# A compression MLP inside an attention layer with its matmul operands exchanged: the weights stand still, the windows stream

## The chip, the core and the metric

The kernel runs on one core of a Trainium2 chip. The metric is the device time of one execution in microseconds; lower is better. Five engines matter here: PE (TensorE), DVE (VectorE), ACT (ScalarE), POOL (GpSimd), and SP, which only issues transfers: all of this kernel's loads, stores and moves between tiles stand in SP's one queue, in the order in which the program issues them.

## What is computed

One forward pass in f32 over 512 tokens of width 1024: an even mixer, an MLP, an odd mixer, an MLP, then a hybrid mixer and a gated MLP. The hybrid mixer's second branch attends, per head, to selected keys, to a window of keys, and to keys and values that were compressed from 32 tokens into one. The change touches only the making of these:

```python
def compress(x, pe, w1, w2):
    B, S, G, dh = x.shape
    nc = (S - CMP_LEN) // CMP_STRIDE + 1
    idx = np.arange(nc)[:, None] * CMP_STRIDE + np.arange(CMP_LEN)[None, :]
    blk = x[:, idx] + pe[None, None, :, None, :]
    blk = blk.transpose(0, 1, 3, 2, 4).reshape(B, nc, G, CMP_LEN * dh)
    return jax.nn.silu(blk @ w1) @ w2
...
    k_cmp = compress(apply_rope(kv(kc_), c3, s3), cmp_pe_k, cmp_k_w1, cmp_k_w2)
    v_cmp = compress(kv(vc_), cmp_pe_v, cmp_v_w1, cmp_v_w2)
```

Here S = 512, G = 2 groups, dh = 64, CMP_LEN = 32, CMP_STRIDE = 16. So there are 31 windows for each of 2 groups, 62 in all; w1 is 2048 x 256 and w2 is 256 x 64. The product with w1 is 62 x 2048 x 256, once for k and once for v.

## The kernel before

The program first records its operations without issuing them (class with `own`, `later`, `schedule`, `issue`), then `schedule()` (L391) simulates the engines with costs of its own and writes out one order per engine; then every operation is issued from one line, L372. So every row of the trace has L372, and tiles are told apart by name. Names with several buffers share a pool (`BUFS`, L544): three of P, G and L, two of strip, wr, wh, wl, one of acc and rbcq; in PSUM three of psg (the pool "g", for projections), two each of pss and psp, one of pso. A tile gets a buffer when the last user of an older one is done. Work recorded under `rec.later(LATER)` is filler: it is recorded ahead, with a lower priority than the attention heads whose waits it is to fill.

A projection ("gemm") works in pieces: a weight piece of 512 KB is loaded to wr; ACT copies it to wh in a narrower float format, DVE writes the rest to wl, and each 128 x 512 result in psg takes 24 matmuls, with wh, wh and wl.

The hybrid mixer (L1211) makes, as filler under the first differential attention heads (L1317 to L1349): the projections vc and kcs (what is to be compressed), kw, then `compress("v")` (L1338), the projection nsa_v (L1340: values of both other branches, in four token tiles), `compress("k")` (L1342), and the first query projection nq0 (L1344). After the next heads come nq1 (L1399), the rest of k's compression (`next(hk)`, L1400), and the gate projection mg0, whose first piece is followed by `cmp_tiles` (L1406), which multiplies the compressed hidden states by w2.

`compress` (L1518) is a generator in two halves. The first writes the windows (two strip tiles of 128 x 496: partition = half of a window's 32 positions x 64 features, columns = 8 positions x 62 windows), loads w1 in eight pieces of 256 KB, alternately to rbcq and acc, and multiplies: 16 steps, each with 62 window columns as the stationary operand and 256 columns of weights moving, into psg[62, 256]. The second half computes y * 1/(1+exp(-y)) on 62 partitions x 256, turns it with two PE transposes into 128 x 62 halves, and copies these into `hid` (a P tile). One f32 matmul appears in the trace as two records of PE, each with its own weight load.

The planner's price for an f32 matmul is `max(4n/2.4, 428)` ns, with n the moving columns (L322 and following).

Of the kernel before, what the change touches and what calls it, by code (L numbers as in the profile page):

```python
# [102 lines left out]
def pack_weights(i):  # L103
    pk = Packer()
    r = np.arange
    w = i["w_in_ab"][0]
    o_q, o_k, o_v, o_f, o_qb, o_kb, o_vb = 0, 512, 1024, 1536, 1544, 2056, 2568
    pk.moving("fox_v0", w, np.concatenate([r(o_v, o_v + 256), r(o_f, o_f + 8)]))
    pk.moving("fox_v1", w, r(o_v + 256, o_v + 512))
    for t in range(4):  # L110
        pk.stationary(f"fox_qk{t}", w, np.concatenate([r(o_q + 128 * t, o_q + 128 * t + 128), r(o_k + 128 * t, o_k + 128 * t + 128)]))
        pk.stationary(f"chk_qk{t}", w, np.concatenate([r(o_qb + 128 * t, o_qb + 128 * t + 128), r(o_kb + 128 * t, o_kb + 128 * t + 128)]))
    pk.moving("chk_v0", w, r(o_vb, o_vb + 256))
    pk.moving("chk_v1", w, r(o_vb + 256, o_vb + 512))
    for h in range(2):
        pk.stationary(f"out_ab{h}", i["w_out_ab"][0][512 * h:512 * h + 512])
        pk.stationary(f"out_cd{h}", i["w_out_cd"][0][512 * h:512 * h + 512])
    for l in range(2):
        for s in range(4):
            pk.stationary(f"up{l}_{s}", i["w_up"][l][:, 1024 * s:1024 * s + 1024])  # L120
            pk.stationary(f"down{l}_{s}", i["w_down"][l][1024 * s:1024 * s + 1024])

    w = i["w_in_cd"][0]
    for t in range(4):
        pk.stationary(f"sb_qk{t}", w, np.concatenate([r(128 * t, 128 * t + 128), r(512 + 128 * t, 640 + 128 * t)]))
    pk.moving("sb_v0", w, r(1024, 1280))
    pk.moving("sb_v1", w, r(1280, 1536))
    pk.stationary("cq", w, r(1536, 1920))
    pk.stationary("ckv", w, r(1920, 2176))
    kr = r(2176, 2208)  # L130
    krs = np.concatenate([kr[16:], kr[:16]])
    pk.stationary("kr", w, np.concatenate([kr, krs, kr, krs]))
    w = i["w_uq"][0]
    hd = r(8)[:, None] * 96
    pk.stationary("uq_rope", w, np.concatenate([(hd + 64 + r(16)[None]).reshape(-1), (hd + 80 + r(16)[None]).reshape(-1)]))
    nope = (hd + r(64)[None]).reshape(-1)
    for t in range(4):
        pk.stationary(f"uq_nope{t}", w, nope[128 * t:128 * t + 128])
    w = i["w_ukv"][0]
    hd = r(8)[:, None] * 128  # L140
    kn = (hd + r(64)[None]).reshape(-1)
    vv = (hd + 64 + r(64)[None]).reshape(-1)
    for t in range(4):
        pk.stationary(f"ukv_k{t}", w, kn[128 * t:128 * t + 128])
    for g in range(2):
        pk.moving(f"ukv_v{g}", w, vv[256 * g:256 * g + 256])

    w = i["w_in_2"][0]
    dq, dk, dv, nq, kc, vc, ks, vs, kw, vw, ng, mg = 0, 512, 1024, 1536, 2048, 2176, 2304, 2432, 2560, 2688, 2816, 2840
    pk.stationary("vc", w, r(vc, vc + 128))  # L150
    halves = lambda o, n, b: (o + r(n)[:, None] * 64 + 32 * b + r(32)[None]).reshape(-1)
    for b in range(2):
        pk.stationary(f"kcs{b}", w, np.concatenate([halves(kc, 2, b), halves(ks, 2, b)]))
    pk.stationary("kw", w, np.concatenate([halves(kw, 2, 0), halves(kw, 2, 1)]))
    pk.moving("nsa_v", w, np.concatenate([r(vs, vs + 128), r(vw, vw + 128), r(ng, ng + 24)]))
    for g in range(2):
        for b in range(2):
            pk.stationary(f"nq{g}{b}", w, halves(nq + 256 * g, 4, b))
            pk.stationary(f"dq{g}{b}", w, halves(dq + 256 * g, 4, b))
            pk.stationary(f"dk{g}{b}", w, halves(dk + 256 * g, 4, b))  # L160
        pk.moving(f"dv{g}", w, r(dv + 256 * g, dv + 256 * g + 256))
    for b in range(2):
        pk.stationary(f"mg{b}", w, r(mg + 1024 * b, mg + 1024 * b + 1024))
    pk.stationary("ya", i["w_branch_a_2"][0])
    pk.stationary("yb", i["w_branch_b_2"][0])
    pk.stationary("out2", i["w_out_2"][0])
    for s, f0 in enumerate(range(0, FF2, 1024)):
        f1 = min(f0 + 1024, FF2)
        pk.stationary(f"gate_{s}", i["w_gate_2"][0][:, f0:f1])
        pk.stationary(f"up2_{s}", i["w_up_2"][0][:, f0:f1])  # L170
        pk.stationary(f"down2_{s}", i["w_down_2"][0][f0:f1])
    for n in "kv":
        w1 = i[f"cmp_{n}_w1_2"][0].reshape(2, 16, 64, 256)
        w1 = np.concatenate([w1[0], w1[1]], axis=1)
        pk.plain(f"cmp1{n}", [w1[l:l + 2].transpose(1, 0, 2).reshape(128, 512) for l in range(0, 16, 2)])
    return pk


# [324 lines left out]
class Net:  # L503
# [709 lines left out]
    def hybrid_mixer(self):  # L1213
# [100 lines left out]
            nc.vector.tensor_scalar(z[:, i], ps[:, 256:280], self.rcol[:, i:i + 1], None, ALU.mult)  # L1314

        with self.rec.later(LATER):
            self.gemm("vc", h, evac_vc)  # L1317
            self.gemm("kcs0", h, evac_kcs)
            self.gemm("kcs1", h, evac_kcs)
            a, b = self.rope(hold[0], hold[1], ck[:, 0], ck[:, 1], None)  # L1320
            raw["k"] = self.rows_of(self.tl("QS", [128, 2, 512]))
            for g in range(2):
                r = slice(32 * g, 32 * g + 32)
                for o, src in ((0, a), (32, b)):
                    nc.sync.dma_start(raw["k"][g][o:o + 32], src[r])
                    nc.sync.dma_start(raw["k"][g][64 + o:96 + o, 0:496], src[r, 16:512])
            sa, sb_ = self.pair("AB"), self.pair("AB")
            self.split(sa[64:128], a[64:128])
            self.split(sb_[64:128], b[64:128])
            for g in range(2):  # L1330
                k = self.pair("KK")
                r = slice(64 + 32 * g, 96 + 32 * g)
                for d in (0, 64):
                    self.move(k[d:d + 32], sa[r])
                    self.move(k[d + 32:d + 64], sb_[r])
                ksel.append(k)
            self.gemm("kw", h, evac_kw)
            hv = self.compress("v", raw["v"])  # L1338
            next(hv)
            vt = self.v_tiles("nsa_v", h, rcol, gates)  # L1340
            hv = next(hv)
            hk = self.compress("k", raw["k"])  # L1342
            next(hk)
            qs0 = self.roped_stacks("nq0", h, cq, "QS")  # L1344
            nc.scalar.activation(z, z, AF.Exp, scale=-1.0)
            nc.vector.tensor_scalar(z, z, 1.0, None, ALU.add)
            nc.vector.reciprocal(gt, z)
            late = self.tl("P", [128, 256])
            nc.sync.dma_start(late, self.ins["late"][:, 256:512])  # L1349
            self.cmask = self.c2("cmask", self.tl("cmask", [128, 128]))  # L1350
# [164 lines left out]
        self.gemm_tok(key, stat, evac)  # L1515
        return res

    def compress(self, n, src):  # L1518

        nc = self.nc  # L1520
        win = []
        for l0 in (0, 8):
            t = self.tl("strip", [128, 8, 2, 31])
            pe = self.v(f"pe{n}")[:, l0:l0 + 8].unsqueeze(2).to_broadcast([128, 8, 31])
            for g in range(2):
                view = src[g][:, 0:496].rearrange("p (c l) -> p l c", l=16)
                nc.vector.tensor_tensor(t[:, :, g], view[:, l0:l0 + 8], pe, ALU.add)
            win.append(t)
        ps = self.psum("g")
        for l in range(16):  # L1530
            if l % 2 == 0:
                off, w = self.pk.index[f"cmp1{n}"][0][l // 2]
                wt = self.tl("acc" if l % 4 else "rbcq", [128, 512])
                nc.sync.dma_start(wt, self.ins["w"][off:off + 128 * w].rearrange("(p c) -> p c", p=128))
            nc.tensor.matmul(ps[0:62, 0:256], win[l // 8][:, l % 8].rearrange("p g c -> p (g c)"),
                             wt[:, 256 * (l % 2):256 * (l % 2) + 256], start=(l == 0), stop=(l == 15))
        yield
        act = self.tl("P", [128, 512])
        e, y = act[0:62, 0:256], act[0:62, 256:512]
        nc.scalar.activation(e, ps[0:62, 0:256], AF.Exp, scale=-1.0)  # L1540
        nc.scalar.activation(y, ps[0:62, 0:256], AF.Copy)
        nc.vector.tensor_scalar(e, e, 1.0, None, ALU.add)
        nc.vector.reciprocal(e, e)
        nc.vector.tensor_tensor(y, y, e, ALU.mult)
        ps = self.psum("g")
        for m in range(2):
            nc.tensor.transpose(ps[:, 64 * m:64 * m + 62], y[:, 128 * m:128 * m + 128], self.c("ident")[0:62, 0:62])
        hid = self.tl("P", [128, 2, 2, 32])
        nc.vector.memset(hid, 0.0)
        for m in range(2):  # L1550
            nc.vector.tensor_copy(hid[:, m, :, 0:31], ps[:, 64 * m:64 * m + 62].rearrange("p (g c) -> p g c", g=2))
        yield hid

    def cmp_tiles(self, hk, hv, late):
# [236 lines left out]
```

## Time and profile before

| | |
|---|---|
| runs of the kernel before | 2073.0, 2075.69, 2075.41 us, median 2075.41 |
| the profiled execution | 2075.91 us; span of the trace 2074.2 us |
| mean granted TensorE clock | 0.991 of full speed |
| busy: PE, its weight loads, DVE, ACT, POOL | 97%, 81%, 55%, 43%, 19% of the span |

How to read it: durations are those of the profiled execution. PE's row counts matmul time, PEld's its weight loads, which overlap with matmuls. A timeline row is a run of equal instructions; in brackets stands how long its engine had been idle before it, and what released it. In an operand list `psg<-rbcq,strip` the tile written comes first, then the moving one, then the stationary one. A tile's two numbers, as in 128*62, are the rows and the columns of the stationary operand. The share of PE leaves 58 us of the span in which it is idle.

### The profile page before, as it was taken

The page shows a single profiled execution, that of the slowest core. Times are in us where ns is not written, and L with a number is a line of the kernel's source. Part 1 is how long each engine was busy: PE and PEld are TensorE (multiplying, and loading weights), DVE is VectorE, ACT ScalarE, POOL GpSimd, SP SyncE. Part 2 cuts the span into 40 slices and gives each one's busy share as a digit, 9 for nine tenths or more (in the row PEclk, how much of TensorE's full clock was granted, in tenths as well). Part 3 has the DMA queues.
Part 4 walks back from the last instruction along what each step waited for, and adds up shares of the span by engine and source line. Part 5 has one row for each costly group of instructions (what it writes and reads, how often), then busy time and mean ns, then how long its engine had stood idle before and what let it go on. Part 6 is the DMA issues. An engine that isn't in the chain of part 4 may idle for free. (4 is left out here: it accounts for less than half of the span.)

```text
span 2074.2 us, 27227 instructions
## 1 busy us (share of the span) xinstructions
PE 2016.1 (97%) x9958; PEld 1684.7 (81%) x9958; DVE 1134.4 (55%) x2033; ACT 895.1 (43%) x1621; POOL 394.3 (19%) x524
## 2 busy tenths in 40 slices
PE   8999999999999998999999999989999999999998
PEld 7887778888888887878888888867788888888887
DVE  6657763434444677874434354766786644333334
ACT  5556542323344565652323253534685543222224
POOL 2343210000022453220000014212240221011013
PEclk9999999999999999999999999999999999999999
DMA  6545623233344325633333334464113222323232
GB/s 199 135 128 152 195 83 102 92 102 92 101 134 132 102 62 130 194 101 96 97 100 94 102 120 141 119 174 126 60 42 112 92 101 92 102 92 102 91 102 82
DMA packets 80677, 231.98 MB, mean 112 GB/s; under 512 B 11552, under 2 KB 15520, under 8 KB 80544
## 3 DMA queue, kind: packets, MB, share of 16 engines
q1 hardware_dynamic: 80544, 230.25, 36.8%
q8 instruction: 78, 1.28, 0.3%
q14 instruction: 55, 0.45, 0.1%
HBM read 183.04 MB, written 10.49 MB: 93 GB/s over the span
## 5 line engine op out<-in xcount | busy, mean ns | idle before, releaser
L372 PE MATMUL psg<-h,wh 128*128 128x512 f32 x2688 | 847.3, 393 | 1.0 <-ACT h L372 0.6
L372 ACT ACTIVATE wh<-wr 128x1024 fp32r<-128x1024 f32 (+3 forms) x313 | 326.2, 1042 | 847.8 <-PE psg L372 679.1
L372 PEld LDWEIGHTS psg<-h,wh 128*128 128x128 f32 x2688 | 503.4, 189 | 101.4 <-ACT h L372 1.1
L372 PE MATMUL psg<-h,wl 128*128 128x512 f32 x1344 | 528.6, 393 | 0.9 <-DVE wl L372 0.7
L372 DVE TENSOR_TENSOR wl<-wr,wh 128x1024 fp32r<-128x1024 f32 (+3 forms) x313 | 385.7, 1233 | 60.7 <-ACT wh L372 59.6
L372 PEld LDWEIGHTS psg<-h,wl 128*128 128x128 f32 x1344 | 253.7, 189 | 53.1 <-DVE wl L372 2.4
L372 DVE TENSOR_TENSOR x<-psg,x 128x512 f32<-128x512 f32 (+1 forms) x120 | 78.1, 654 | 281.9 <-PE psg L372 281.9
L372 PE MATMUL psg<-KK,wh 128*128 128x512 f32 (+1 forms) x752 | 226.3, 382 | 0.0
L372 POOL TENSOR_TENSOR acc<-acc,T 128x512 f32<-128x512 f32 (+1 forms) x50 | 73.5, 1470 | 776.6 <-issue 629.1
L372 PE MATMUL psg<-V,wh 128*128 128x512 f32 (+1 forms) x656 | 200.4, 386 | 0.0
L372 PEld LDWEIGHTS psg<-KK,wh 128*128 128x128 f32 x752 | 140.0, 188 | 27.5
L372 PE MATMUL psg<-KK,wl 128*128 128x512 f32 (+1 forms) x376 | 143.8, 382 | 0.0
L372 PEld LDWEIGHTS psg<-V,wh 128*128 128x128 f32 x656 | 122.8, 188 | 25.0
L372 DVE SCALAR_TENSOR_TENSOR T<-psg,rbc 128x512 f32<-128x512 f32 x64 | 44.3, 692 | 167.8 <-PE psg L372 167.2
L372 PE MATMUL psg<-o,wh 128*128 128x512 f32 x400 | 131.8, 399 | 3.4 <-DVE AB L372 1.5
L372 ACT ACTIVATE x<-x,sm 128x128 f32<-128x128 f32 (+1 forms) x192 | 106.5, 558 | 55.9 <-DVE sm L372 55.5
L372 PE MATMUL psg<-V,wl 128*128 128x512 f32 (+1 forms) x328 | 126.7, 386 | 0.0
L372 PE MATMUL psg<-wh,h 128*128 128x256 f32 (+2 forms) x560 | 113.8, 290 | 6.9 <-ACT wh L372 6.8
L372 PE MATMUL pso<-pt,V 128*128 128x128 f32 (+3 forms) x432 | 108.1, 337 | 2.7 <-ACT pt L372 1.3
L372 POOL TENSOR_SCALAR x<-x,sm 128x128 f32<-128x128 f32 (+1 forms) x112 | 65.4, 589 | 178.5 <-DVE sm L372 100.2
L372 PEld LDWEIGHTS psg<-wh,h 128*128 128x128 f32 x560 | 91.6, 193 | 8.8 <-ACT wh L372 6.8
L372 POOL TENSOR_TENSOR T<-T,rbc 128x512 f32<-128x512 f32 x22 | 39.2, 1781 | 280.5 <-ACT T L372 280.5
(267 smaller groups left out, 2701.4 us busy)
## 6 DMA issues: line engine op xcount, KB each, us to landing
wr<-in_w_dram SPq DMA_DIRECT2D x302, 512.0 KB, 3.5
KK<-AB SPq DMA_DIRECT2D x48, 256.0 KB, 5.6
QS<-AB SPq DMA_DIRECT2D x48, 128.0 KB, 3.8
x<-xs SPq DMA_DIRECT2D x24, 256.0 KB, 3.3
xs<-P SPq DMA_DIRECT2D x16, 256.0 KB, 3.5
xs<-x SPq DMA_DIRECT2D x16, 256.0 KB, 2.0
h<-AB SPq DMA_DIRECT2D x16, 256.0 KB, 3.8
KK<-AB SPq DMA_DIRECT2D x32, 128.0 KB, 2.3
```

The source lines that it names most:

```text
L372: op.inst = getattr(getattr(nc, op.eng), op.name)(*op.args, **op.kw)
```

## The change

w1 is packed anew, as four blocks of 128 x 1024 (512 KB) instead of eight of 128 x 512; each block holds 8 positions for one half (128) of the 256 hidden columns. The blocks go to the three 4 KB buffers of L, which so far only the odd mixer uses. The loads are recorded by a new function, `cmp_weight`: three of v's ahead of the projections, two of k's ahead of nsa_v, the others where their matmuls come. The windows go to the single buffers rbcq and acc, which the weights had. The matmuls exchange their operands: 128 x 128 of weights stand, 62 columns of windows move; there are 32 for each of k and v instead of 16. Their result is 128 x 62, hidden columns on the partitions, so that the two transposes and the two copies go. The activations work on 128 partitions: four of 128 x 62 instead of two of 62 x 256, a reciprocal of 128 x 128 instead of 62 x 256, and two products written straight into `hid`. `hid` is now taken before `act`, both from P, and `act` is cleared too.

```diff
-        pk.plain(f"cmp1{n}", [w1[l:l + 2].transpose(1, 0, 2).reshape(128, 512) for l in range(0, 16, 2)])
+        pk.plain(f"cmp1{n}", [w1[l:l + 8, :, m:m + 128].transpose(1, 0, 2).reshape(128, 1024) for m in (0, 128) for l in (0, 8)])
...
         with self.rec.later(LATER):
+            wv = [self.cmp_weight("v", b) for b in range(3)]
             self.gemm("vc", h, evac_vc)
...
-            hv = self.compress("v", raw["v"])
+            hv = self.compress("v", raw["v"], wv)
             next(hv)
+            wk = [self.cmp_weight("k", b) for b in range(2)]
             vt = self.v_tiles("nsa_v", h, rcol, gates)
             hv = next(hv)
-            hk = self.compress("k", raw["k"])
+            hk = self.compress("k", raw["k"], wk)
...
+    def cmp_weight(self, n, b):
+        off, w = self.pk.index[f"cmp1{n}"][0][b]
+        t = self.tl("L", [128, 1024])
+        self.nc.sync.dma_start(t, self.ins["w"][off:off + 128 * w].rearrange("(p c) -> p c", p=128))
+        return t
...
-            t = self.tl("strip", [128, 8, 2, 31])
+            t = self.tl("acc" if l0 else "rbcq", [128, 512])[:, 0:496].rearrange("p (l g c) -> p l g c", l=8, g=2)
...
-        for l in range(16):
-            if l % 2 == 0:
-                off, w = self.pk.index[f"cmp1{n}"][0][l // 2]
-                wt = self.tl("acc" if l % 4 else "rbcq", [128, 512])
-                nc.sync.dma_start(wt, self.ins["w"][off:off + 128 * w].rearrange("(p c) -> p c", p=128))
-            nc.tensor.matmul(ps[0:62, 0:256], win[l // 8][:, l % 8].rearrange("p g c -> p (g c)"),
-                             wt[:, 256 * (l % 2):256 * (l % 2) + 256], start=(l == 0), stop=(l == 15))
+        for m in range(2):
+            for l in range(16):
+                b = 2 * m + l // 8
+                if b == len(ws):
+                    ws.append(self.cmp_weight(n, b))
+                c = 128 * (l % 8)
+                nc.tensor.matmul(ps[:, 64 * m:64 * m + 62], ws[b][:, c:c + 128],
+                                 win[l // 8][:, l % 8].rearrange("p g c -> p (g c)"), start=(l == 0), stop=(l == 15))
         yield
-        act = self.tl("P", [128, 512])
-        e, y = act[0:62, 0:256], act[0:62, 256:512]
-        nc.scalar.activation(e, ps[0:62, 0:256], AF.Exp, scale=-1.0)
-        nc.scalar.activation(y, ps[0:62, 0:256], AF.Copy)
+        act = self.tl("P", [128, 2, 128])
+        e, y = act[:, 0], act[:, 1]
+        hid = self.tl("P", [128, 2, 2, 32])
+        nc.vector.memset(hid, 0.0)
+        nc.vector.memset(act, 0.0)
+        for m in range(2):
+            c = slice(64 * m, 64 * m + 62)
+            nc.scalar.activation(e[:, c], ps[:, c], AF.Exp, scale=-1.0)
+            nc.scalar.activation(y[:, c], ps[:, c], AF.Copy)
         nc.vector.tensor_scalar(e, e, 1.0, None, ALU.add)
         nc.vector.reciprocal(e, e)
-        nc.vector.tensor_tensor(y, y, e, ALU.mult)
-        ps = self.psum("g")
         for m in range(2):
-            nc.tensor.transpose(ps[:, 64 * m:64 * m + 62], y[:, 128 * m:128 * m + 128], self.c("ident")[0:62, 0:62])
-        hid = self.tl("P", [128, 2, 2, 32])
-        nc.vector.memset(hid, 0.0)
-        for m in range(2):
-            nc.vector.tensor_copy(hid[:, m, :, 0:31], ps[:, 64 * m:64 * m + 62].rearrange("p (g c) -> p g c", g=2))
+            c = slice(64 * m, 64 * m + 62)
+            nc.vector.tensor_tensor(hid[:, m, :, 0:31], y[:, c].rearrange("p (g c) -> p g c", g=2),
+                                    e[:, c].rearrange("p (g c) -> p g c", g=2), ALU.mult)
         yield hid
```

Because the order is planned from costs and buffers, rows move that the diff does not name. In the rows of the planned order a tile has a number, x8 means eight instructions in a row, and the listing's shapes are those of the tile written.

**SP's queue from v's compression to k's.** Before, from the load of v's third piece on (KK and wr belong to the key copies and the next projections):

```order
L372 DMA rbcq_2470<-in_w_dram 128x512
L372 DMA acc_2471<-in_w_dram 128x512
L372 DMA wr_2505<-in_w_dram 128x1024
L372 DMA wr_2509<-in_w_dram 128x1024
L372 DMA KK_2463<-AB_2462 32x1024 x4
L372 DMA KK_2464<-AB_2462 32x1024 x4
L372 DMA rbcq_2472<-in_w_dram 128x512
L372 DMA acc_2473<-in_w_dram 128x512
```

Changed, from the load of v's fourth block (L_2471) to k's last (L_2494); v's first three stand much earlier, in the odd mixer:

```order
L373 DMA L_2471<-in_w_dram 128x1024
L373 DMA wr_2496<-in_w_dram 128x1024
L373 DMA wr_2500<-in_w_dram 128x1024
L373 DMA L_2472<-in_w_dram 128x1024
L373 DMA KK_2466<-AB_2465 32x1024 x4
L373 DMA KK_2467<-AB_2465 32x1024 x4
L373 DMA L_2473<-in_w_dram 128x1024
L373 DMA L_2493<-in_w_dram 128x1024
L373 DMA wr_2604<-in_w_dram 128x1024
L373 DMA wr_2608<-in_w_dram 128x1024
L373 DMA L_2494<-in_w_dram 128x1024
```

v's pieces that stood behind the eight KK moves are gone from there. k's last block stands behind the two wr pieces of nq1 (wr_2604 and wr_2608).

**PE from k's compression to nq0.** Before, the last six k groups and nq0's first result, psg_2504, alternate; k's result is psg_2495:

```order
L372 MATMUL psg_2495<-acc_2501,strip_2494 62x256 x2
L372 MATMUL psg_2504<-h_2203,wl_2507 128x512
L372 MATMUL psg_2504<-h_2210,wh_2506 128x512 x2
L372 MATMUL psg_2504<-h_2210,wl_2507 128x512
L372 MATMUL psg_2504<-h_2217,wh_2506 128x512 x2
L372 MATMUL psg_2504<-h_2217,wl_2507 128x512
L372 MATMUL psg_2504<-h_2224,wh_2506 128x512 x2
L372 MATMUL psg_2504<-h_2224,wl_2507 128x512
L372 MATMUL psg_2495<-rbcq_2502,strip_2494 62x256 x2
L372 MATMUL psg_2495<-acc_2503,strip_2494 62x256 x2
L372 MATMUL psg_2508<-h_2177,wh_2510 128x512 x2
```

Changed (psg_2486 is the last tile of nsa_v, psg_2492 k's result, psg_2495 now nq0's first):

```order
L373 MATMUL psg_2486<-wh_2478,h_2224 128x280
L373 MATMUL psg_2486<-wl_2479,h_2224 128x280
L373 MATMUL psg_2486<-wh_2478,h_2224 128x280
L373 MATMUL psg_2492<-rbcq_2490,L_2472 128x62 x8
L373 MATMUL psg_2492<-acc_2491,L_2473 128x62 x8
L373 MATMUL psg_2492<-rbcq_2490,L_2493 128x62 x8
L373 MATMUL psg_2492<-acc_2491,L_2494 128x62 x8
L373 MATMUL psg_2495<-h_2177,wh_2497 128x512 x2
```

All 32 matmuls of k's compression stand between nsa_v and nq0. k's result is read by ACT only at the place that follows, so that its psg buffer stays taken until then; nq1's first result, psg_2603, follows psg_2495 and psg_2499 with a wait for DVE, which it had not before.

**PE and DVE at `cmp_tiles`.** Before (psg_2638 and psg_2641: v's tiles for the two groups, from strip and w2 in P_2520; pso and psp belong to an attention head):

```order
L372 MATMUL psg_2632<-h_2224,wl_2635 128x512
L372 MATMUL psg_2638<-P_2520,strip_2637 128x64 x2
L372 MATMUL pso_2707<-pt_2669_2741,V_2483 128x512 [waits Activation_49]
L372 MATMUL psp_2744<-cst,x_2735 128x128 [waits DVE_49,PE_49]
L372 MATMUL psp_2744<-cst,x_2738 128x128
L372 MATMUL pso_2707<-pt_2669_2741,V_2483 128x512
L372 MATMUL pso_2707<-pt_2671_2743,V_2485 128x384 [waits Activation_49]
L372 MATMUL psp_2746<-cst,x_2738 128x128 [waits DVE_49,PE_49]
L372 MATMUL pso_2707<-pt_2671_2743,V_2485 128x384
L372 MATMUL pso_2707<-pt_2673_2745,V_2487 128x256 [waits Activation_49]
L372 MATMUL pso_2707<-pt_2673_2745,V_2487 128x256 [waits DVE_49]
```

Changed, PE (psg_2628 and psg_2631 are v's tiles, psg_2633 k's, P_2620 k's `hid`):

```order
L373 MATMUL psg_2622<-h_2224,wl_2625 128x512
L373 MATMUL psg_2628<-P_2511,strip_2627 128x64 x2
L373 MATMUL psg_2631<-P_2511,strip_2630 128x64 [waits DVE_49]
L373 MATMUL psg_2631<-P_2511,strip_2630 128x64
L373 MATMUL psg_2633<-P_2620,P_2511 64x64 [waits DVE_49] x2
L373 MATMUL psg_2636<-o_2385,wh_2638 128x512 [waits Activation_49]
L373 MATMUL psg_2636<-o_2385,wh_2638 128x512
```

Changed, DVE at the same place (P_2489 is v's `hid`, P_2619 k's `act`):

```order
L373 COPY strip_2630<-P_2489 128x2x32 [waits PE_49]
L373 TENSOR_TENSOR wl_2644<-wr_2642,wh_2643 128x1024 [waits DMAHW2_49,Activation_49]
L373 TENSOR_TENSOR vcmp_2557_2629<-psg_2628,vcmp_2557_2629 128x64 [waits Activation_49]
L373 COPY strip_2630<-P_2489 128x2x32 x3
L373 SCALAR_TENSOR_TENSOR V_2621<-V_2621,G_2626 128x512 [waits DVE_49,Activation_49]
L373 MEMSET P_2619 128x256 [waits DVE_49]
L373 TENSOR_SCALAR P_2619<-P_2619 128x128 [waits DVE_49,Activation_49]
L373 TENSOR_TENSOR vcmp_2560_2632<-psg_2631,vcmp_2560_2632 128x64 [waits Activation_49]
L373 RECIPROCAL P_2619<-P_2619 128x128 [waits DVE_49]
L373 TENSOR_TENSOR P_2620<-P_2619 128x2x31 [waits DVE_49]
L373 TENSOR_TENSOR P_2620<-P_2619 128x2x31
```

The attention matmuls that stood between v's two tiles stand earlier now. k's sigmoid, which ran during nq0 and nq1 before, stands between v's second tile and k's product with w2: P_2619 takes the buffer of P_2489, which the copies to strip_2630 read last.

## Rows read from the trace of the kernel before

**Rows 1.** The page, part 1: busy time, share of the span, instructions of TensorE and its weight loads.
```profile
PE 2016.1 (97%) x9958; PEld 1684.7 (81%) x9958; DVE 1134.4 (55%) x2033; ACT 895.1 (43%) x1621; POOL 394.3 (19%) x524
```

**Rows 2.** Stretches of 20 us: busy us of each engine (x instructions), granted clock, DMA share, GB/s.
```profile
1380.00:1400.00 20.00, 13.97 (x85) 11.04 (x83) 10.28 (x37) 7.13 (x19) 2.45 (x4) 0.92 0.61 166
...
1460.00:1480.00 20.00, 19.02 (x86) 15.41 (x84) 11.23 (x39) 7.32 (x23) 1.67 (x3) 0.83 0.19 63
```

**Rows 3.** Timeline of PE, 1372 to 1401: start, duration, group, [idle before <-releaser].
```profile
1372.58 1.08 PE L372 MATMUL psg<-rbcq,strip 128*62 128x256 f32 x4 [1.33 <-DVE strip L372]
...
1374.44 0.40 PE L372 MATMUL psg<-wh,h 128*128 128x280 f32 x1
...
1383.67 1.07 PE L372 MATMUL psg<-rbcq,strip 128*62 128x256 f32 x4 [0.61 <-DMA rbcq<-in_w_dram]
...
1391.32 0.29 PE L372 MATMUL psg<-wh,h 128*128 128x280 f32 x1
1396.93 1.96 PE L372 MATMUL psg<-rbcq,strip 128*62 128x256 f32 x4 [5.32 <-DMA rbcq<-in_w_dram]
...
1400.33 0.74 PE L372 MATMUL pss<-o,X 128*128 128x512 f32 x2
```

**Rows 4.** Timeline of SP's DMA queue, 1381 to 1395: start, time in the queue, transfers.
```profile
1383.63 10.24 SPq L372 DMA_DIRECT2D KK<-AB  x8
1393.96 0.53 SPq L372 DMA_DIRECT2D rbcq<-in_w_dram  x1
```

**Rows 5.** Timeline of PE: small moving tiles, each with the next matmul behind it.
```profile
1416.49 0.94 PE L372 MATMUL pss<-cst,T 128*128 128x1 f32 x8
1417.30 0.48 PE L372 MATMUL psg<-h,wl 128*128 128x512 f32 x1
...
1457.78 0.55 PE L372 MATMUL psg<-P,strip 128*128 128x64 f32 x4
...
1458.31 0.49 PE L372 MATMUL pso<-pt,V 128*128 128x512 f32 x1
```

**Rows 6.** Groups by form, 1365 to 1470, PE: busy us, mean ns | idle before, releaser.
```profile
L372 PE MATMUL psg<-cst,P 62*128 62x62 f32 x4 | 0.9, 258 | 0.0
```

**Rows 7.** The page, part 6: issues, KB each, median us to landing.
```profile
wr<-in_w_dram SPq DMA_DIRECT2D x302, 512.0 KB, 3.5
```

**Rows 8.** Timelines of DVE, ACT and SP around one split of a weight tile.
```profile
1410.61 1.05 ACT L372 ACTIVATE wh<-wr 128x1024 fp32r<-128x1024 f32 x1
...
1411.63 1.21 DVE L372 TENSOR_TENSOR wl<-wr,wh 128x1024 fp32r<-128x1024 f32 x1
...
1412.90 0.33 SPq L372 DMA_DIRECT2D wr<-in_w_dram  x1
...
1426.48 0.69 DVE L372 TENSOR_TENSOR G<-psg,X 128x512 f32<-128x512 f32 x1 [3.39 <-PE psg L372]
```

**Rows 9.** Timeline of all engines, 1459 to 1465, in which k's and v's compressed tiles are made.
```profile
1459.41 0.41 PE L372 MATMUL psp<-cst,x 128*128 128x128 f32 x2 [0.61 <-DVE pt L372]
...
1459.88 1.22 DVE L372 TENSOR_TENSOR wl<-wr,wh 128x1024 fp32r<-128x1024 f32 x1
...
1461.49 0.90 PE L372 MATMUL pso<-pt,V 128*128 128x256 f32 x3 [0.78 <-DVE pt L372]
...
1461.55 0.68 DVE L372 SCALAR_TENSOR_TENSOR V<-V,G 128x512 f32<-128x512 f32 x1
...
1462.59 1.12 PE L372 MATMUL psg<-P,strip 128*128 128x64 f32 x4 [0.20 <-DVE strip L372]
...
1463.64 0.69 PE L372 MATMUL psg<-P,P 128*64 128x64 f32 x4
...
1463.75 0.22 ACT L372 ACTIVATE vcmp<-psg 128x64 fp32r<-128x64 f32 x1 [0.86 <-PE psg L372]
```

**Rows 10.** Groups by form, 1365 to 1470, DVE: busy us, mean ns | idle before, releaser.
```profile
L372 DVE RECIPROCAL P<-P 62x256 f32<-62x256 f32 x2 | 3.4, 1713 | 0.0
```

**Rows 11.** Timeline of PE in the odd mixer, where its three L tiles come free.
```profile
849.09 0.93 PE L372 MATMUL pss<-h,h 96*128 96x128 f32 x6 [2.18 <-DMA h<-AB]
```

More of the change, by code (lines that the diff above doesn't have):

```diff
@@ L1516, in wide_v, with compress @@
         return res
-    def compress(self, n, src):
+    def cmp_weight(self, n, b):
[3 more added lines that the diff above has]
+        return t
+    def compress(self, n, src, ws):
         nc = self.nc
```

## The prediction

> **What bounds the kernel now.** The page's first part says that PE is busy for 97% of the span [rows 1]. So time is won only where PE does less or stands idle, and lost only where PE is made to wait. A difference under about 0.2% (4 us) can't be told from no change here.
>
> The windows over 1380 to 1480 show where PE idles near the change: 6.03 of the 20 us from 1380, and 0.98 from 1460, where the clock is granted at 0.83 [rows 2]. The timeline says why [rows 3]. At 1391.32 PE runs out of work and sits 5.32 us until a rbcq piece of v's weights lands; 0.61 us at 1383.67 have the same releaser. SP's queue shows that this piece was not slow but late: its turn came at 1393.96, behind eight KK moves that held the queue for 10.24 us [rows 4]. The idle stretch costs twice: after it the eight f32 records take 1400.33 - 1396.93 = 3.40 us, where eight took 1374.44 - 1372.58 = 1.86 at the start of v; the clock behind the wait is at half (1.2 GHz), 1.54 us lost. So 5.32 + 0.61 + 1.54 = 7.5 us hang on late weights.
>
> **The matmuls.** Before: 64 records at 1.86 / 8 = 0.2325 us, 14.9 in all at full clock. After: 128 records, each with a load of 128 weight columns and 62 moving columns. The nearest rows: 128 x 128 f32 with one moving column, eight from 1416.49 to 1417.30, 0.101 each; with 64 columns, four from 1457.78 to 1458.31, at most 0.133 each [rows 5]. One column costs three quarters of what 64 do, so the weight load sets the pace. 128 x 0.101 = 12.9 and 128 x 0.133 = 17.0; I take 0.11, nearer to the longer run of eight: 14.1. **Term: -0.8 us, from -2.0 to +2.1.** Double the instructions, a quarter of the columns, the same time.
>
> The four transpose records go: 258 ns each, overlapping [rows 6]; at the pace of the one-column rows 0.1 each. **Term: -0.4.** The four activations more are short (one of 128 x 64 took 0.22 [rows 9]) and ACT is at 43% [rows 1]: nothing by themselves. The reciprocal falls from 1.71 us [rows 10] to about half (128 of 256 columns, 0.86): DVE is at 55%, nothing where it runs under nq0, but it counts below.
>
> **v and nsa_v.** The three blocks of v loaded in the odd mixer are there long before, and the fourth stands before the eight KK moves: the 7.5 us go. Given back: v's matmuls alternated with nsa_v, and both covered the first head's chain of softmax, transposes and products. Now v's matmuls come first and are its only cover. From 1374.44 to 1391.32 stand 54 records of nsa_v [rows 3], 6.9 us at some 0.13 a record (280 columns at 2.4 GHz are 0.12); with 16 of v's records, 3.7 us, that is 10.6 us of cover. After, it is v's 7.05, so 3.5 less. If PE only queued behind filler, nothing is lost (0); if the chain keeps the pace it had, 3.5, and up to 1 more because PE's order is fixed and a wait holds what stands behind it. I take 3: nearly each chain row of PE waits for DVE or ACT in the planned order. **Term: -7.5 + 3.0 = -4.5, from -7.5 to -3.0.**
>
> **k.** k's 32 matmuls stand in one piece after nsa_v. The last block, L_2494, stands in SP's queue behind wr_2608, and this waits for a wr buffer, which is free when wl of nq0's second piece is written, and that needs a wl buffer of nsa_v. From nsa_v's end: evacuation 0.69 (like that of G), wh 1.05, wl 1.21, two issues of 0.33 [rows 8], landing 3.5 [rows 7]: 7.1 us. In the rows the wr issue follows wl's end by 0.06. Three groups of k cover 48 x 0.11 = 5.3. **Term: +1.8, from 0 (if the split starts in nsa_v's last tile) to +3.**
>
> **The psg buffer.** k's result keeps one of three buffers until after nq1, so nq1's first result waits for the two readings of psg_2499 by DVE, 0.69 each [rows 8], and a margin for the hand-over, which no row isolates: **+1.6, from 0 (covered) to +3.3** (if it gets psg_2495's buffer, whose second reader stands behind these, a wl of 1.21 and takes 0.69 itself).
>
> **cmp_tiles.** Before, 4.3 us went from v's first tile to its second (1458.31 to 1462.59), with attention between them, and k's product followed at 1463.64: 5.3 us [rows 5, 9]. After, nothing stands between, and k's sigmoid hangs on the release of v's `hid`. DVE from the first tile on: wl 1.22, two copies and v's difference 0.6, one product 0.68 [rows 9], the memset 0.2, four activations of 0.22 on ACT, an addition 0.3, the reciprocal 0.86, two products 0.35: 5.1, and with hand-overs between PE, DVE, ACT, DVE and PE, which I put at 0.35 each, some 6.5 us. PE's own two tiles cover 1.5 of it, so it idles 5.0. Before, it idled 0.61 + 0.78 + 0.20 = 1.6 here [rows 9]. That is 3.4 more; the attention work moved forward fills some wait of its old neighbours, so I take **+3.0, from +2.0 to +4.5.** In the window with these waits the clock was granted at 0.83 already [rows 2]; a longer stop may keep it at half longer, by what the wait at 1391 cost: **+0.7, from 0 to 1.5.**
>
> **Odd mixer.** Three loads of 512 KB enter SP's queue where the L tiles come free, where PE already waits 2.18 us for a move of h [rows 11]. An issue of a load stayed 0.33 us in the queue [rows 8]; three before such a move are 1 us, none 0, and the transfers share the memory. **+0.5, from -1 (another order, by chance better) to +2.**
>
> **Sum:** -0.8 - 0.4 - 4.5 + 1.8 + 1.6 + 3.7 + 0.5 = **+1.9 us** on the profiled execution's 2075.9. That execution stands 0.5 above the median of the three runs, 2075.4, so I forecast 2077.3: no change that can be measured, with a lean to slower.
>
> **A rule to weigh.** By the one-column rows a record with 128 weight columns takes 0.101 us, however few columns move [rows 5]. The Trainium skill ("TensorE: Matmul & The Clock Gate", section "Back-to-back issue gap") gives an isolated gap of about 60 cycles for 1 to 64 moving columns; by 25 ns a record the 128 would be 3.2 us, and by that the sum would be -9.0, 2066.4. The one-column row contradicts this for f32 with a new weight tile each time, so it is a rival of small chance, below.
>
> **Rivals.**
>
> *A, slower: k's sigmoid on the critical path.* k's hidden state has no slack left; its memset waits for DVE's copies, and PE has nothing else in its order. For it: the planned rows at `cmp_tiles`, and the psg buffer. Against it: attention work moved forward may cover elsewhere. It decides once what it adds, with the buffer and L_2494, passes the 5.7 us won at matmuls, transposes and v by over 4. With cmp_tiles at +4.5 and 1.5 of clock, the buffer at 3.3, the wait for L_2494 at 3 and v at -3.0: -1.2 - 3.0 + 3 + 3.3 + 6 + 0.5 = +8.6, about 2084.0.
>
> *B, faster: late weights were the whole matter.* The 7.5 us come through, because the chain kept its pace only by queueing behind filler, and the waits behind are short: -0.8 - 0.4 - 7.5 + 0.5 + 0.5 + 2 = -5.7, about 2069.7. For it: the 5.32 us are one clean wait [rows 3, 4], and three blocks now land 500 us early. Against it: each of the new waits would have to come in at its low end.
>
> *C, faster: moving columns set the time.* 62 of 256 columns of 0.2325 us are 0.056 a record, 7.2 us in all instead of 14.1: the sum falls to -5.0, about 2070.4. The one-column row speaks against it. This is the case that the rule above is nearest to.
>
> *D, the change does not do what it says.* The planner prices an f32 matmul at no less than 428 ns, so 64 of them count 27 us for it where the rows say 14; it may have placed all else for a PE that is later than it is, and the wait for DMA only moves, from v's rbcq to k's L_2494, at 5 us and half clock after it: -1.2 - 4.5 + 5 + 1.5 + 1.6 + 3.7 + 0.5 = +6.6, 2082.0.
>
> **How the numbers follow.** My forecast (within 0.2%) 0.42; A 0.20 and D 0.13, both slower, 0.33 together; B 0.20 and C 0.05, both faster, 0.25. The range goes from below B to above A, since these hold more than half of the chance and neither end can be left out: 2067.5 to 2085.5. The likeliest case alone would be 2071.3 to 2079.5.
>
> **What would show it.** Right: PE's records of psg<-rbcq,L and psg<-acc,L start 0.10 to 0.13 us apart; no PE wait for a weight DMA in v, a short one before k's last group; a wait for DVE before psg of nq1; idle of some 5 us before psg<-P,P, released by DVE P. Wrong: records under 0.08 or over 0.15 us apart; gaps in v over 5 us; psg<-P,P starting without a wait; or a difference of over 3 us that lies before 1365 or after 1480.

## The result and the profile after

| | before | changed |
|---|---|---|
| median of 17 runs, us | 2073.0 (2066.5 to 2077.4) | 2084.2 (2080.2 to 2096.3) |
| ratio, 95% interval | | 1.0064, 1.0050 to 1.0079 |
| profiled execution: span, mean granted clock | 2074.2, 0.991 | 2094.4, 0.983 |

The change makes the kernel slower by 0.64%, some 13 us. The forecast was no measurable change. The page of the changed kernel, part 1, answers to [rows 1]:

```profile
PE 2028.8 (97%) x10018; PEld 1706.6 (81%) x10018; DVE 1134.1 (54%) x2033; ACT 895.1 (43%) x1625; POOL 394.4 (19%) x524
```

PE is busier by 12.7 us, although it has less to stream: the first sign that its time at half clock grew, and not its work.

The profiled execution of the change was the slowest of its 17, and 3.5 us of its distance lie before 846 us, where both kernels issue the same orders; 7.9 in all have come together by the end of kw. The prediction named a difference of over 3 us ahead of 1365 as a sign of being wrong. It isn't shown to come from the change: some 0.7 of it arises where the three early loads stand (840 to 856), and with the same loads v starts 1.4 and 4.4 us earlier than before in the profiles of e2 and e8 (below). From the end of kw the distance grows to 20.1 us at 1490, and stays there to the end. So the change is worth about +12.2 us in the stretch of compression, which agrees with the ratio. Over the 17 runs of the change the time follows the mean granted clock: 0.981 to 0.985 in the six slowest (2088.6 us and more), 0.984 to 0.988 in the others.

PE's timeline of v, k and nq0's start (start, duration, group, [idle before <-releaser]), against [rows 3]:

```profile
1380.82 1.55 PE L373 MATMUL psg<-rbcq,L 128*128 128x62 f32 x12 [1.67 <-DVE rbcq L373]
1383.92 0.69 PE L373 MATMUL psp<-cst,x 128*128 128x128 f32 x2 [1.55 <-DVE x L373]
...
1392.58 1.05 PE L373 MATMUL pss<-cst,T 128*128 128x1 f32 x8 [0.53 <-ACT T L373]
1393.49 1.94 PE L373 MATMUL psg<-rbcq,L 128*128 128x62 f32 x8
...
1403.40 0.58 PE L373 MATMUL psg<-wh,h 128*128 128x280 f32 x1
...
1422.78 1.90 PE L373 MATMUL psg<-rbcq,L 128*128 128x62 f32 x16
1424.52 1.95 PE L373 MATMUL psg<-acc,L 128*128 128x62 f32 x16
1426.30 1.95 PE L373 MATMUL psg<-rbcq,L 128*128 128x62 f32 x16
1432.45 3.67 PE L373 MATMUL psg<-acc,L 128*128 128x62 f32 x16 [4.20 <-DMA L<-in_w_dram]
1435.88 1.20 PE L373 MATMUL psg<-h,wh 128*128 128x512 f32 x2
```

No wait for a weight is left in v. But after 12 of v's records PE waits 1.55 us for the attention chain, and by then the clock falls. The stretches of 2 us of the same kernel (columns as in [rows 2]) show what follows:

```profile
1384.00:1386.00 2.00, 2.00 (x10) 1.90 (x10) 1.94 (x4) 0.98 (x2) 0.00 (x0) 0.50 0.14 34
...
1394.00:1396.00 2.00, 2.00 (x12) 2.00 (x11) 0.00 (x0) 0.00 (x0) 0.93 (x1) 0.50 0.83 225
...
1400.00:1402.00 2.00, 2.00 (x11) 1.90 (x10) 1.45 (x9) 1.20 (x4) 0.48 (x1) 0.50 1.00 227
...
1408.00:1410.00 2.00, 2.00 (x18) 2.00 (x17) 0.20 (x2) 0.35 (x1) 0.00 (x0) 1.00 0.00 0
...
1424.00:1426.00 2.00, 2.00 (x21) 2.00 (x19) 2.00 (x4) 1.09 (x3) 0.00 (x0) 1.00 0.74 258
...
1434.00:1436.00 2.00, 2.00 (x11) 2.00 (x11) 0.00 (x0) 0.00 (x0) 0.00 (x0) 0.50 0.00 0
```

From 1383.9 to 1390 and from 1393.5 to 1407 PE is busy without a gap at half clock (1.2 GHz). It rises at 1407; nsa_v's first matmuls stand from 1403.4 on. Before, the clock behind the 5.32 us wait was at half for some 3.4 us. The records themselves cost what was forecast: at full clock 16 from 1422.78 to 1424.52, 0.109 us each; at half clock 16 from 1432.45 to 1435.88, 0.214.

k's last 16 waited 4.20 us. SP's queue shows why:

```profile
1392.30 8.55 SPq L373 DMA_DIRECT2D KK<-AB  x8
...
1423.34 2.67 SPq L373 DMA_DIRECT2D wr<-in_w_dram  x2
1426.11 0.38 SPq L373 DMA_DIRECT2D L<-in_w_dram  x1
```

L_2494, the last row, was issued behind nq1's two pieces, 3.3 us after nsa_v's end, and landed 6.3 us later, where the median of pieces of 512 KB before is 3.5 [rows 7]. Two such pieces were in flight in front, which can't be all of it: the three had moved nearly all their bytes by 1430, and then little came (DMA share 0.05, 18 GB/s):

```profile
1430.00:1432.00 2.00, 0.00 (x0) 0.00 (x0) 0.00 (x0) 0.00 (x0) 0.00 (x0) 0.76 0.05 18
```

What held the rest is open. After the wait the clock was at half until 1441.3; nq0's first result took 1443.96 - 1435.88 = 8.1 us instead of 5.5.

Further on, nq1's first result and `cmp_tiles`, against [rows 9]:

```profile
1451.04 0.70 PE L373 MATMUL psg<-h,wh 128*128 128x512 f32 x2 [1.47 <-DVE G L373]
...
1479.70 0.66 PE L373 MATMUL psg<-P,strip 128*128 128x64 f32 x4 [2.23 <-DVE strip L373]
1483.17 0.69 PE L373 MATMUL psg<-P,P 128*64 128x64 f32 x4 [2.81 <-DVE P L373]
1483.79 1.22 PE L373 MATMUL psg<-o,wh 128*128 128x512 f32 x2
```

The buffer wait (1.47 us), and a stop of 2.23 and one of 2.81 for DVE, where before there were 0.61, 0.78 and 0.20: 5.0 us of idle time for 1.6, as forecast.

### The profile page after: what moved, and what is told of

It reads as the page before. It is cut to its first block, busy times and chain, and to the rows that moved or that the text cites. A ratio compares the mean times of both kernels' runs of the same rounds, so it can differ in the third digit from the quotient of the medians.

```text
span 2094.4 us, 27344 instructions
## 1 busy us (share of the span) xinstructions
PE 2028.8 (97%) x10018; PEld 1706.6 (81%) x10018; DVE 1134.1 (54%) x2033; ACT 895.1 (43%) x1625; POOL 394.4 (19%) x524
```

## The experiments

To read the profiles alike, I cut from each the stretch from v's first record to the first psg<-o,wh behind k's product with w2, and summed PE over windows of 1 us: idle, and the time lost to the clock, as busy time x (1 - granted clock). These three columns are of one execution each. Attention work that the planner puts in or out of the stretch shifts its length by a few us. The ratio is to the kernel before, on the same chip.

| kernel | ratio, 95% interval | stretch | idle | lost to clock |
|---|---|---|---|---|
| before | 1 | 91.7 | 9.6 | 2.8 |
| the change | 1.0064 (1.0050 to 1.0079) | 103.0 | 14.1 | 14.7 |
| e1 operands alone | 1.0008 (0.9990 to 1.0026) | 92.9 | 8.9 | 6.7 |
| e2 blocks alone | 0.9978 (0.9961 to 0.9996) | 83.0 | 3.8 | 0.5 |
| e3 price | 0.9973 (0.9953 to 0.9992) | 85.5 | 7.1 | 3.6 |
| e4 act first | 1.0027 (1.0008 to 1.0045) | 94.7 | 7.7 | 12.2 |
| e5 price, v only | 1.0044 (1.0027 to 1.0062) | 94.5 | 9.4 | 10.5 |
| e6 price, k only | 1.0033 (1.0020 to 1.0047) | 93.3 | 9.8 | 8.7 |
| e7 before with e3's price | 0.9996 (0.9983 to 1.0009) | 90.9 | 8.5 | 2.2 |
| e8 price, act first | 0.9940 (0.9920 to 0.9960) | 77.9 | 2.3 | 0.0 |
| e9 columns twice | 1.0060 (1.0042 to 1.0077) | 98.7 | 15.7 | 6.8 |
| e10 columns four times | 1.0058 (1.0040 to 1.0076) | 97.5 | 8.8 | 0.3 |
| e11 price, v and k | 1.0012 (0.9994 to 1.0030) | 90.8 | 8.0 | 8.8 |
| e12 e8, columns twice | 0.9933 (0.9914 to 0.9951) | 78.2 | 2.2 | 0.0 |

The change against before: +4.5 idle, +11.9 clock, and 5.1 less of other work in the stretch.

**e1 and e2: which half of the change costs?** e1 keeps the old loads and exchanges the operands. It has the change's sigmoid on 128 partitions, but with `act` taken before `hid`:

```diff
-            nc.tensor.matmul(ps[0:62, 0:256], win[l // 8][:, l % 8].rearrange("p g c -> p (g c)"),
-                             wt[:, 256 * (l % 2):256 * (l % 2) + 256], start=(l == 0), stop=(l == 15))
+            for m in range(2):
+                c = 256 * (l % 2) + 128 * m
+                nc.tensor.matmul(ps[:, 64 * m:64 * m + 62], wt[:, c:c + 128],
+                                 win[l // 8][:, l % 8].rearrange("p g c -> p (g c)"), start=(l + m == 0), stop=(l + m == 16))
```

> The kernel before with its 256 KB pieces of weights in rbcq and acc, its windows in strip and its order of loads; only the operands are exchanged (each piece is used as 128 x 128 blocks, both halves of the hidden columns into one psg tile), with the sigmoid on 128 partitions and act taken before hid. Theory 1 (the exchanged matmuls cost no more as such; the loss of the change comes from where they stand: all of v's ahead of nsa_v, where PE's clock falls to half at the first wait of the attention chain, and from the late last block of k): v's groups alternate with nsa_v as before, so -2 to +3 us to the kernel before, with the 5 us wait for rbcq still there. Theory 2 (the exchanged f32 records are dear wherever they stand, because the clock stays at half while they run): +8 us or more, the clock at half for more than 10 us between v's start and nq0.

e2 keeps the new loads and the old operands, and the old sigmoid with its transposes (shown against the kernel before):

```diff
+            b = l // 4
+            if b == len(ws):
+                ws.append(self.cmp_weight(n, b))
             nc.tensor.matmul(ps[0:62, 0:256], win[l // 8][:, l % 8].rearrange("p g c -> p (g c)"),
-                             wt[:, 256 * (l % 2):256 * (l % 2) + 256], start=(l == 0), stop=(l == 15))
+                             ws[b][:, 256 * (l % 4):256 * (l % 4) + 256], start=(l == 0), stop=(l == 15))
```

> The change's four 512 KB blocks in the L tiles, loaded as early as there, with the windows in rbcq and acc, but the old operands: 62 window columns stand, 256 columns of weights move; sigmoid, transposes and copies as before. Theory 1: the wait for late weights (7.5 us with the clock) goes, v's matmuls stand partly ahead of nsa_v, k's last block may wait a little: -8 to -2 us to the kernel before. Theory 3 (what costs is the loads and the L tiles: three loads into the odd mixer, the last block late): +5 us or more, like the change.

Neither half is slow. e1 gives +0.08%, as theory 1 said; theory 2 (dear records wherever they stand) falls, though e1 already loses 3.9 us more to the clock than before. In its timeline a wait for rbcq is still there, though shorter than 5.32:

```profile
1374.87 1.10 PE L372 MATMUL psg<-strip,rbcq 128*128 128x62 f32 x8 [1.38 <-DVE strip L372]
...
1396.31 1.07 PE L372 MATMUL psg<-strip,rbcq 128*128 128x62 f32 x8 [2.79 <-DMA rbcq<-in_w_dram]
```

e2 gives -0.22%, 4.6 us, as theory 1 said; theory 3 falls. It too has v's first records in one piece ahead of nsa_v, but 12 of them last 2.8 us instead of 1.55, so the chain behind them is nearly ready, and the clock holds:

```profile
1371.21 2.80 PE L373 MATMUL psg<-L,rbcq 128*62 128x256 f32 x12 [1.67 <-DVE rbcq L373]
...
1374.32 0.44 PE L373 MATMUL psp<-cst,x 128*128 128x128 f32 x2 [0.31 <-DVE x L373]
```

So what costs is the two together, or what neither half has: `hid` taken before `act`. e3 and e4 take these apart.

**e3, e5, e6, e7, e11: the planner's price.** One number is altered:

```diff
-                return max(4 * n / 2.4, 428)
+                return max(4 * n / 2.4, 214)
```

> The change with one number of the planner altered: an f32 matmul counts at least 214 ns instead of 428 ns (two records at 0.109 us are 218). In its order v's last 8 matmuls alternate with nsa_v and k's with a chain of attention; at cmp_tiles the sigmoid of k still stands between v's and k's products. Theory 1: less of v stands alone and k's last block is covered better: 3 to 9 us better than the change, that is +4 to +10 us to the kernel before. Theory 2: as the change, +11 to +15.

e3 is 0.27% faster than before and some 19 us better than the change, where I had expected 3 to 9. Its order puts v's last records into nsa_v, k's second block too ahead of the eight KK moves, and k's matmuls into an attention chain. e5 and e6 give a price of 218 ns to v's or k's matmuls only, e11 to both; e7 is the control.

> The change with the planner's price of 218 ns for v's 32 matmuls alone. In its order v's last 8 stand in nsa_v, and k's are spread over an attention chain too, though their price is still 428. Theory 1a (what the price mends is the place of v's matmuls): most of e3's gain, -6 to +1 us to the kernel before, the clock at half for less than 6 us between v and nq0 (in the change some 25). Theory 1b (it is k's late last block): +6 us or more.

> The same price for k's 32 matmuls alone. v's still stand all ahead of nsa_v, k's in one piece behind it, k's last block one place earlier in SP's queue. Theory 1a: +8 to +13 us to the kernel before, v's half clock as in the change. Theory 1b: the wait before k's last eight is below 2 us and the result is +5 us or less.

> The kernel before with e3's number (214 ns at least for every f32 matmul). Its matmuls of compression have 256 columns and keep their 427 ns; only small f32 matmuls elsewhere (sums with one column, products with w2) count less. If e3 gained by the compression's order: -2 to +2 us. If by the other small matmuls: -4 us or more, and then e3 says little about the change.

> The change with the price of 218 ns for v's and k's matmuls of compression and for no others. e3 had it for all small f32 matmuls. If the gain of e3 is the place of these 64: -8 to 0 us to the kernel before. If it came from other small matmuls or from chance in the order: as e5 and e6, +6 to +10.

e7 shows no gain by the price alone. e5 and e6 each bring back a part (0.20% and 0.31% of the change's 0.64%), and e11 about their sum and no more (0.52%), as if the two places were separate losses. e5's +9 us fits theory 1b and e6's +7 neither, so both were too simple. e6 shows k's part: its last block stands one place earlier in SP's queue, and the last 16 records start 2.54 us behind the third group's, where 1.74 is their pace; 0.8 us is left of the wait of 4.20:

```profile
1419.84 1.95 PE L377 MATMUL psg<-rbcq,L 128*128 128x62 f32 x16
...
1422.38 1.98 PE L377 MATMUL psg<-acc,L 128*128 128x62 f32 x16
```

e5 still loses 10.5 us to the clock, in v and again at k. e11, at +2.5 us, lies between its two expectations, so the place of these 64 matmuls is not all of e3's gain. e3 beats e11 by some 8 us, with an order that differs in when other small f32 matmuls run; by which of them isn't settled.

**e4: k's sigmoid and its buffer.**

```diff
         act = self.tl("P", [128, 2, 128])
         e, y = act[:, 0], act[:, 1]
-        hid = self.tl("P", [128, 2, 2, 32])
-        nc.vector.memset(hid, 0.0)
         nc.vector.memset(act, 0.0)
...
         nc.vector.reciprocal(e, e)
+        hid = self.tl("P", [128, 2, 2, 32])
+        nc.vector.memset(hid, 0.0)
```

> The change with act taken from P before hid, so that k's act does not wait for v's hid to be released: k's sigmoid runs under nq0, the psg buffer of k's result comes free before nq1, and attention matmuls stand between v's two tiles again. The trace of the change against that of before gives 1.6 us for the psg buffer and 2.8 us for cmp_tiles with the clock behind it: both go, 3 to 5 us better than the change, +7 to +10 us to the kernel before; v's half clock and the 4.2 us wait for k's last block stay. If the sigmoid was not on the path: no better than the change.

+0.27% instead of +0.64%: 7.7 us, more than the 3 to 5 expected (by the two intervals some 3 to 13, an estimate). So more than half of the change's loss goes with these two lines. The stops before nq1, v's second tile and k's product are gone from the timeline; the wait for k's last block is not:

```profile
1425.57 3.67 PE L373 MATMUL psg<-acc,L 128*128 128x62 f32 x16 [4.11 <-DMA L<-in_w_dram]
```

**e9 and e10: more columns through the same order.** The clock was named as the cost; it can be tried without touching an order. The windows stream twice or four times through the same weights, and ACT reads the first copy of the result (the lines of e10):

```diff
-                nc.tensor.matmul(ps[:, 64 * m:64 * m + 62], ws[b][:, c:c + 128],
-                                 win[l // 8][:, l % 8].rearrange("p g c -> p (g c)"), start=(l == 0), stop=(l == 15))
+                nc.tensor.matmul(ps[:, 256 * m:256 * m + 248].rearrange("p (a c) -> p a c", a=4), ws[b][:, c:c + 128],
+                                 win[l // 8][:, l % 8].rearrange("p g c -> p (g c)").unsqueeze(1).to_broadcast([128, 4, 62]),
+                                 start=(l == 0), stop=(l == 15))
```

> The change in its own order on every engine, but each of the 128 records of compression streams its 62 window columns twice (124 columns, the second half of the result is not read). At full clock 124 columns of f32 are about 0.11 us by the 256 columns in 0.2275, no more than the 128-column weight load in front (0.109 in the change), so the records should keep their spacing. Theory 4a (PE's clock stays at half in v and after k's wait because little streams through it in these stretches): the clock is at full for more of v, the result 2 to 8 us better than the change, +5 to +10 us to the kernel before, although PE does more. Theory 4b (only the waits matter, not what runs between them): as the change, +11 to +15, clock rows alike.

> As e9 with 248 columns, the window columns four times. A record then takes 0.22 us at full clock (256 columns took 0.2275), so the 128 records cost 28 us instead of 14 at full clock, and about 0.43 each at half. Theory 4a: the clock holds full through v, the extra 14 us of work are partly paid back by some 12 us that the change loses to the clock: +8 to +18 us to the kernel before. Theory 4b: half clock as in the change for the same stretches, records of 0.43 there: +25 us or more.

e10 streams for 13 us more (128 records, 0.21 us apart instead of 0.109) and takes the time of the change:

```profile
1414.77 3.52 PE L373 MATMUL psg<-rbcq,L 128*128 128x248 f32 x16
1418.13 3.52 PE L373 MATMUL psg<-acc,L 128*128 128x248 f32 x16
```

And its windows, to be read beside those of the change above (v starts at 1376.0 here, at 1380.8 there), all have full clock, where that had half in the first three:

```profile
1384.00:1386.00 2.00, 2.00 (x13) 1.82 (x13) 2.00 (x4) 0.00 (x0) 0.00 (x0) 1.00 0.32 70
...
1394.00:1396.00 2.00, 2.00 (x12) 1.63 (x10) 1.90 (x9) 0.71 (x3) 0.10 (x1) 1.00 1.04 227
...
1400.00:1402.00 2.00, 2.00 (x18) 2.00 (x17) 2.00 (x6) 1.00 (x3) 0.00 (x0) 1.00 0.95 385
...
1424.00:1426.00 2.00, 2.00 (x11) 1.81 (x10) 0.43 (x1) 0.00 (x0) 0.00 (x0) 1.00 0.00 0
```

In its stretch 14.4 us of lost clock and 5.3 of idle are gone, which pays for the streaming: theory 4b, with half clock in the same stretches and +25 us, falls. But the pair does not set the clock apart from the waits. Both have one order, yet the longer records of e10 also cover: the wait behind v's first 12 records is 0.32 us instead of 1.55, as in e2, and k's wait of 4.20 is gone. The clock by itself is seen where a wait stayed. The first line is e9's, where the change had 1.55; the others are e10's, and at the last of them the change had 0.53, with 13 us at half clock behind it:

```profile
1377.82 0.44 PE L373 MATMUL psp<-cst,x 128*128 128x128 f32 x2 [1.50 <-DVE x L373]
...
1379.12 0.44 PE L373 MATMUL psp<-cst,x 128*128 128x128 f32 x2 [0.32 <-DVE x L373]
...
1388.04 1.05 PE L373 MATMUL pss<-cst,T 128*128 128x1 f32 x8 [0.73 <-ACT T L373]
```

The granted clock was 1.00 behind each of these three; in e9 it fell only at 1388.5. So in these profiles the length of the wait does not set the loss. Nor is e10's one lucky profile: the granted clock was 0.990 to 0.994 in its six runs, 0.981 to 0.988 in the 17 of the change. How much of the change's 13 us is the clock by itself, no run isolates. On time e9 is less clear: twice the columns are free (0.111 us a record), 7.9 us of clock come back in its profile, but PE then waits more (15.7 us), 3.88 of it for k's last block as before; the stretch is 4.3 us shorter, the runs are no better than the change's, at +12.4 us against 4a's +5 to +10.

```profile
1413.87 1.95 PE L373 MATMUL psg<-rbcq,L 128*128 128x124 f32 x16
1415.65 1.95 PE L373 MATMUL psg<-acc,L 128*128 128x124 f32 x16
...
1423.27 3.78 PE L373 MATMUL psg<-acc,L 128*128 128x124 f32 x16 [3.88 <-DMA L<-in_w_dram]
```

**e8 and e12: the better version.** Price and act first together:

> e3 and e4 together: the planner's price of 214 and act taken before hid. If the two losses are separate (place of the matmuls; k's sigmoid and its psg buffer), e4's gain of some 4 us or more comes on top of e3: -7 to -12 us to the kernel before, no PE wait for DVE P before k's product with w2 and none for DVE G before nq1. If they overlap: as e3, -3 to -7.

0.60% faster than before, some 12 us, and 25 better than the change. The two losses are separate: the price is worth 19 us with `hid` first and 18 with `act` first, `act` first 7.7 us at the old price and 6.8 at the new. In its profile, of the fastest of its six runs, the granted clock is 1.00 through the whole stretch, and no wait for DVE P is left:

```profile
1360.00:1380.00 20.00, 17.94 (x121) 15.86 (x120) 19.72 (x38) 8.91 (x18) 5.30 (x5) 1.00 0.52 144
1380.00:1400.00 20.00, 20.00 (x155) 19.29 (x153) 16.95 (x59) 11.85 (x33) 3.42 (x5) 1.00 0.67 196
1400.00:1420.00 20.00, 20.00 (x122) 17.76 (x121) 8.53 (x16) 4.88 (x10) 2.24 (x2) 1.00 0.22 79
1420.00:1440.00 20.00, 19.45 (x97) 15.73 (x96) 15.04 (x41) 10.80 (x27) 10.59 (x12) 1.00 0.44 125
1440.00:1460.00 20.00, 18.73 (x102) 15.00 (x101) 13.51 (x47) 10.04 (x28) 1.66 (x3) 1.00 0.28 87
```

```profile
1445.13 0.66 PE L373 MATMUL psg<-P,strip 128*128 128x64 f32 x4
1445.72 0.45 PE L373 MATMUL psg<-P,P 128*64 128x64 f32 x4
1446.09 0.73 PE L373 MATMUL psg<-o,wh 128*128 128x512 f32 x2
```

> e8 (price 214, act before hid) with the window columns streamed twice as in e9, in e8's own order. e8's profile shows no half clock at all between v's start and the product with w2, so there is nothing left for more columns to win: theory 4 in either form gives e8's -9 to -15 us to the kernel before, at most 2 us beside it. If e8's result hung on a clock that happened to hold in its profile and not in its other runs, the doubled columns make it better, -15 us or more.

0.67% faster: the same, and no help from more columns where the clock holds already.

## Why the prediction was wrong

- **What bounds the kernel, and the 7.5 us of late weights:** right. With e2's early blocks the wait is gone and the clock stays up; its runs gained 4.6 us.
- **The matmuls:** right, 0.109 us a record for my 0.11. Rival C (0.056) was rightly put low: the records go at the pace of a 128-column weight load, as 62 and 124 columns at one pace show. The Trainium skill ("TensorE: Matmul & The Clock Gate", section "LDWEIGHTS") has columns / 1.2 ns for a weight load, from which I estimate 107 ns for 128. The rows agree at full clock, with 0.109 us; at half clock they have 0.214. The 25 ns a record of the prediction are the isolated gap of the Trainium skill ("TensorE: Matmul & The Clock Gate", section "Back-to-back issue gap"), which by that section under-counts for a stream with weight loads; the rows have 0.109 us.
- **v and nsa_v, -4.5, is the step that failed.** I gave back 3.0 us for lost cover and put the clock at nothing, without a reason. In the rows PE idled 1.55 and 0.53 us in v, less than the 3 allowed, but 7 and 13 us at half clock followed, which cost 9.9 us of PE's time (3.1 and 6.8): 12.0 us where the sum has 3.0. Where I priced the clock at all (cmp_tiles, A, D), I gave it at most 1.5 us, read off one case: 1.54 behind a wait of 5.32 with 256-column records. With the same order and more columns, e9 held full clock behind a wait of 1.50 us and e10 behind one of 0.73.
- **k, +1.8, failed in the same way:** the wait was 4.2 us, as the landing took 6.3 where I took the median 3.5; and half clock behind it cost 4.3 us (1.7 in k's last 16 records, 2.6 in nq0), which weren't in the sum. From the end of kw to nq0's second result (1428.24 before, 1443.96 changed) the distance grew from 7.9 to 15.7 us, by +7.8; my terms for this part come to -3.9. The excess over the terms of v and k (9.0 and 6.7) is larger than these 11.7 us; what covers the rest isn't isolated.
- **The psg buffer, +1.6:** 1.47 in the trace. **cmp_tiles, +3.7:** from nq1's start to the end of the stretch and the clock behind it the distance grew by 2.9. Both right by the trace; that they mattered is shown by e4, which gained 7.7 us for these 4.4. **Odd mixer, +0.5:** no run tests it.
- **Rivals.** A's mechanism came true: e4 takes it out and wins 7.7 of the 13 us. That A's 2084.0 meets the measured 2084.2 is luck all the same, as it was reached with 3.3 for the buffer, 6 for cmp_tiles and -3.0 for v. D named the other part: I wrote that the planner prices these matmuls at no less than 428 ns, 27 us for 64 where the rows say 14, and that k's wait moves to L_2494, and gave it 0.13. The doubt was in the text, and I did not work out what a planner that believes PE is busy twice as long does with v's matmuls. e3 shows that this number turns the change's sign. B took the waits behind to be short; k's was 4.2 us, and v's had the half clock behind them.

## What to carry to other kernels

When an edit changes what an instruction costs and a planner orders the program, correct its price in the same edit: here one number was worth more than the edit. Put a price on the clock behind every new wait on PE, and a range on it: here the clock was at half for 7 to 13 us behind waits of 0.5 to 4.2 us in the change, and before for 3.4 behind one of 5.3, and for 6.8 at `cmp_tiles` with waits of 0.2 to 0.8. A median landing is no bound: here a load behind two others of its size took 6.3 us for 3.5.

## What was not expected of the hardware

The clock stayed at half for 13 us while PE's row showed no idle time (1394 to 1407), and held full for the 5.3 us of k's first 48 records of the same kind, which followed nsa_v. At half clock a record of 128 weight columns took 0.214 us for 0.109, so the pace of the weight loads falls with it. At full clock 62 and 124 columns cost the same, 0.109 and 0.111, and 248 cost 0.21. When the clock falls at a short wait is not settled: e5 and e8 begin v alike, 22 records and then a wait of 0.44 us, and e5's profile has half clock from 1373 to 1380, e8's none. The runs of e5, e6, e9 and e10 are some 5 to 6 us slower than the stretches of their profiles suggest. For e5 the profiled execution was the second fastest of 12, and the five slowest had a lower clock (0.982 to 0.985 for 0.989); for the others why is open.
